# Gated panels of three feed-forward blocks transposed by DMA in two 16-bit planes instead of by TensorE, with two adaLN weight streams moved later

## The chip, the cores and the metric

The kernel runs on one core of one Trainium2 chip. The metric is the device time of one execution in microseconds (us). The core has five engines that each work through their own queue in a fixed order: TensorE (PE in the profile, with its weight loads as PEld), VectorE (DVE), ScalarE (ACT), GpSimd (POOL) and SyncE (SP). SP issues nearly all DMAs here. A queue's order is fixed when the program is built. An instruction that must wait holds up everything behind it on its own engine.

## What is computed

The program is a two-layer diffusion backbone over 256 latent tokens (with 256 context tokens in the first feed-forward block and the attention), width 1024, hidden width 2816, float32:

```python
def modulate(x, shift, scale):
    return x * (1 + scale) + shift

def swiglu_ffn(h, w_in, w_out):
    a, u = jnp.split(h @ w_in, 2, axis=-1)
    return (jax.nn.silu(a) * u) @ w_out

def half_step_ffn(x, shift, scale, gate, w_in, w_out, g, b):
    y = swiglu_ffn(modulate(x, shift, scale), w_in, w_out)
    return post_norm_update(x, y, gate, 0.5, g, b)     # LayerNorm(alpha * x + 0.5 * gate * y)
```

Each layer is a feed-forward half step, a token mixer (attention in layer 0, a short gated convolution in layer 1) and a second feed-forward half step. The nine modulation vectors of a layer come from `silu(c) @ ada_w[i] + ada_b[i]`.

## The kernel before, in words

**Precision.** Every float32 matrix product is made of three products of split operands. A number is split into a part `hi` that TensorE takes at its fast rate and the rest `lo = x - hi`, and hi·hi, hi·lo and lo·hi are summed. So each weight that lands from HBM (`w1r`, `w2r`: raw) is split by one ScalarE copy into `w1h` or `w2h` (line 211) and one VectorE subtraction into `w1l` or `w2l` (line 214). A *unit* is 256 rows by 512 columns of weights, 512 KB, and is split in two halves, so in two instructions on each engine.

**A feed-forward block (`ffn`).** Three of the four blocks go through `ffn`: the second of layer 0 (block A here), the first of layer 1 (B) and the second of layer 1 (C). A block has two stages.

The *panel stage* multiplies the modulated tokens by `ffn_w_in` in 11 panels of 256 hidden columns, with 4 units to a panel and two token tiles t = 0, 1 of 128 tokens. A *step* is one unit times one token tile: six matmuls of 128x512. `panels` calls `tick()` after every step; all clocks of the program count steps. The panel stage has 88 steps. When a panel of a token tile is complete, `gated.done` takes `silu` on ScalarE (line 494) and multiplies by the other half on VectorE (line 495), into a tile `sil` with tokens on the partitions. The next product needs the hidden columns on the partitions. So, four steps (`G_LAG`) after both token tiles of a panel are done, `rest` transposes the panel with four TensorE transposes of 128x128 into a PSUM bank `gT` (line 503), and `finish` splits that bank into `gh` (ScalarE, line 113) and `gl` (VectorE, line 114).

The *output stage* multiplies these by `ffn_w_out` in 22 units (two column halves of 11). Its 44 steps are put in order by `order_skew`: token tile 1 follows tile 0 at a distance of five units. Counting steps of this stage from 0, unit u is first used at step 2u-5 (from u = 5 on) and last used at step 2u+6. At the stage's end come the residual (`res`), the layer norm and the transposes for the next block.

**Buffers.** There are four raw unit buffers, five pairs `hi`/`lo` in a pool of the whole program, and as many further pairs as `ext[0]` says. It is 3 in blocks A, B, C and the convolution, so that 8 pairs are used in turn: unit u can be split once unit u-8 has been used for the last time.

**The modulation streams (`ada`).** Background generators load `ada_w` in row blocks of 512 KB (`ar`, three buffers, line 316 on SP), and VectorE adds each, times a column of `silu(c)`, to a sum `acc` in two halves (lines 295 and 297). After eight blocks GpSimd sums over the partitions (`red`, line 307) and adds the result to a row in HBM (`scr`, line 308). `set_background(gen, rate, hold)` makes `rate` generator steps per step of the product, after `hold` steps. A stream of two vectors has 17 such steps. Block A runs the stream for vectors 4 and 5 of layer 1 (rate 0.35, hold 20), block B that for 6 and 7 (rate 0.25), block C that for 8 (rate 0.15). `drain()` runs what is left of a stream. `fold_cols` reads such rows back from `scr` into a small tile `mrow` (line 376, on SP) for the next layer norm but one.

**What sets the order.** TensorE's order is the program's. The other queues are ordered by a list scheduler from priorities when the program is built, so an instruction may stand there long before or after its place in the program. `Late(n, fn)` runs `fn` n steps later. `queued(ins)` places an instruction behind given ones of its queue.

Of the kernel before, what the change touches and what calls it, by code (L numbers as in the profile page):

```python
# [11 lines left out]
F32R = mybir.dt.float32r  # L12
AF = mybir.ActivationFunctionType
# [41 lines left out]
G_LAG = 4  # L55
ROPE_EARLY = 70
# [11 lines left out]
HOLD = 20  # L68
# [3 lines left out]
def backbone_kernel(  # L72
# [19 lines left out]
    w_early = [0]  # L92
    ext = [1, 0]
# [86 lines left out]
    def wunit(srcs, kn, s, own=None, wd=512, put_off=False):  # L180
# [23 lines left out]
        with tc.high_priority(offset=w_early[0]):  # L204
            for src, c in srcs:
                sync.dma_start(rv[:, :, c:c + src.shape[2]], src)

        def parts():
            m = kn * wd
            for a in range(0, m, m // W_HI):  # L210
                nc.scalar.activation(hi[:, a:a + m // W_HI], raw[:, a:a + m // W_HI], AF.Copy)  # L211
            for a in range(0, m, m // W_LO):
                b = a + m // W_LO
                nc.vector.tensor_tensor(out=lo[:, a:b], in0=raw[:, a:b], in1=hi[:, a:b].bitcast(F32), op=ALU.subtract)  # L214
            return hv, lv
# [268 lines left out]
    def run(gen):  # L484
        for _ in gen:
            pass

    def gated(func, finish, s):

        part, res = {}, []  # L490

        def done(p, t, bk):
            g = sp.tile([P, 256], F32, tag="s2", bufs=S2, name=nm("sil"))
            nc.scalar.activation(g, bk[:, 0:256], func)
            gate_ins[:] = [nc.vector.tensor_tensor(out=g, in0=g, in1=bk[:, 256:512], op=ALU.mult)]
            part[p, t] = g
# [344 lines left out]
    def ffn(hTs, later, l, j, i, gm, nxt, own=()):  # L841
# [5 lines left out]
        done, gT = gated(AF.Silu, finish, "gT")  # L847
# [7 lines left out]
        drain()  # L855
# [334 lines left out]
    run(panels(cols, w, hTs, lead_in(6), done, "wc"))  # L1190
    g, hTs, later = sub_end(sc_w_out[0], lhs_T(yT), KC, 1, 1, 5, 1.0, (1, 6), "wo", order_late(KU))
# [57 lines left out]
```

## Time and profile before

| | |
|---|---|
| median of 3 runs | 1258.37 us (1257.19 to 1258.66) |
| the profiled execution's own time | 1258.45 us |
| its span in the trace | 1256.7 us |
| granted TensorE clock over the span | 0.998 of full speed |
| block A: panel stage, output stage | from 592.1 us, from 718.35 us |
| block B: panel stage, output stage | from 780.2 us, from 906.4 us |
| block C: panel stage, output stage | from 1062.7 us, from 1188.5 us |

The profiled execution lies 0.08 us above the median and 1.75 us above its span. The page gives the busy time of each engine, the span in 40 slices, the chain of instructions that ended last, and the costliest groups of instructions. The groups' rows have line, engine, operation, output<-inputs, shape and count, then the busy time in us and the mean of one in ns, then the engine's idle time just before them and what ended it. Rows of the timeline have start and length in us, then the engine, line and operation with a count; idle time before it stands in square brackets, with what ended it. Rows by windows have the busy time of PE, PEld, DVE, ACT and POOL, the granted clock, the busy share of the DMA engines and GB/s.

### The profile page before, as it was taken

To read this page: it belongs to the slowest core of one execution; us is meant where nothing else is said; L and a number is where in the kernel's file an instruction comes from. 1 tells how busy PE (TensorE), PEld (TensorE's weight loads), DVE (VectorE), ACT (ScalarE), POOL (GpSimd) and SP (SyncE) were. 2 spreads that over 40 slices of the span, in tenths; PEclk is the share of its full clock that TensorE was granted. 3 is DMA by queue.
4 is the path that set the end of the run, shared out by engine and by line. 5 is a ranking of instruction groups with operands and counts; after the bars stand their busy time and mean duration, and the time that the engine had idled before them with its cause. 6 is when DMAs were issued, how large, how long until landed. Compare 5 with 4: busy or idle time off the path is not lost.

```text
span 1256.7 us, 17284 instructions
## 1 busy us (share of the span) xinstructions
PE 1241.4 (99%) x5902; PEld 1006.9 (80%) x5902; DVE 966.5 (77%) x1675; ACT 590.2 (47%) x1152; POOL 85.0 (7%) x83
## 2 busy tenths in 40 slices
PE   8999999999999999999999999999999999999997
PEld 6787778778878878777888888888888887888886
DVE  3599987888878877789899646998646788878546
ACT  2432132312326556688655435655435744655431
POOL 0000000000001111120003100021100000002000
PEclk9999999999999999999999999999999999999999
DMA  9976678788842744455899645889645764885641
GB/s 308 299 235 226 197 236 290 265 260 274 285 156 85 216 94 87 99 115 179 259 335 318 231 150 167 274 293 321 224 146 167 245 206 134 259 290 185 227 159 53
DMA packets 202928, 268.59 MB, mean 214 GB/s; under 512 B 30246, under 2 KB 149534, under 8 KB 202840
## 3 DMA queue, kind: packets, MB, share of 16 engines
q1 hardware_dynamic: 202644, 267.46, 67.4%
q8 instruction: 46, 0.75, 0.2%
q14 instruction: 42, 0.34, 0.1%
q0 software_dynamic: 160, 0.02, 0.0%
q10 hardware_dynamic: 36, 0.02, 0.0%
HBM read 265.27 MB, written 2.20 MB: 213 GB/s over the span
## 4 chain that ended last, share of the span: by engine, by line
PE 92%; ACT 3%; DVE 3%; issue 1%; DMA 1%; POOL 0%; DVEq 0%; SPq 0%; POOLq 0%; ACTq 0%
PE f L695 19%; PE w L165 17%; PE w L168 17%; PE w L166 17%; PE wkv L165 2%; PE wkv L166 2%; PE wkv L168 2%; PE wc L165 2%; PE wc L168 2%; PE wc L166 2%; PE gT L503 1%; PE ada L624 1%; PE hT L437 1%; PE S L987 1%; PE wo L165 1%
## 5 line engine op out<-in xcount | busy, mean ns | idle before, releaser
L211 ACT ACTIVATE w1h<-w1r 128x512 fp32r<-128x512 f32 (+1 forms) x352 | 200.0, 620 | 180.0 <-PE w L168 81.5
L214 DVE TENSOR_TENSOR w1l<-w1r,w1h 128x512 fp32r<-128x512 f32 (+1 forms) x352 | 241.7, 734 | 35.5 <-ACT w1h L211 33.2
L165 PE MATMUL w<-w1h,hTh 128*128 128x512 f32 x528 | 209.1, 396 | 1.3 <-ACT hTh L113 1.3
L166 PE MATMUL w<-w1l,hTh 128*128 128x512 f32 x528 | 205.9, 390 | 0.3 <-DVE w1l L214 0.3
L297 DVE SCALAR_TENSOR_TENSOR acc<-ar,cst,acc 128x512 f32<-128x512 f32 x266 | 186.2, 747 | 15.3 <-DMA ar<-in_ada_w_dram 15.3
L165 PE MATMUL w<-w2h,gh 128*128 128x512 f32 (+1 forms) x446 | 173.4, 389 | 0.0
L166 PE MATMUL w<-w2l,gh 128*128 128x512 f32 (+1 forms) x446 | 172.1, 387 | 0.0
L211 ACT ACTIVATE w2h<-w2r 128x512 fp32r<-128x512 f32 x176 | 101.5, 624 | 145.2 <-PE w L168 106.5
L214 DVE TENSOR_TENSOR w2l<-w2r,w2h 128x512 fp32r<-128x512 f32 x176 | 114.1, 688 | 72.0 <-ACT w2h L211 71.2
L168 PE MATMUL w<-w1h,hTl 128*128 128x512 f32 x528 | 163.1, 390 | 0.2 <-DVE hTl L114 0.2
L168 PE MATMUL w<-w2h,gl 128*128 128x512 f32 (+1 forms) x446 | 136.1, 386 | 0.0
L695 PE MATMUL f<-h0h,w1h 128*128 128x512 f32 x352 | 133.1, 394 | 0.4 <-DVE h0h L650 0.4
L695 PE MATMUL f<-h0l,w1h 128*128 128x512 f32 x352 | 133.2, 391 | 0.0
L695 PE MATMUL f<-h0h,w1l 128*128 128x512 f32 x352 | 132.7, 390 | 0.0
L165 PEld LDWEIGHTS w<-w1h,hTh 128*128 128x128 f32 x528 | 99.2, 188 | 21.8 <-ACT hTh L113 2.1
L168 PEld LDWEIGHTS w<-w1h,hTl 128*128 128x128 f32 x528 | 98.9, 188 | 22.0 <-DVE hTl L114 1.0
L166 PEld LDWEIGHTS w<-w1l,hTh 128*128 128x128 f32 x528 | 99.2, 188 | 20.4 <-DVE w1l L214 0.7
L165 PEld LDWEIGHTS w<-w2h,gh 128*128 128x128 f32 x446 | 83.8, 188 | 19.3 <-issue 1.7
L166 PEld LDWEIGHTS w<-w2l,gh 128*128 128x128 f32 x446 | 83.8, 188 | 16.6
L168 PEld LDWEIGHTS w<-w2h,gl 128*128 128x128 f32 x446 | 83.3, 188 | 17.1
L695 PEld LDWEIGHTS f<-h0h,w1h 128*128 128x128 f32 x352 | 65.7, 188 | 19.0 <-issue 4.2
L695 PEld LDWEIGHTS f<-h0l,w1h 128*128 128x128 f32 x352 | 65.5, 188 | 14.4 <-issue 0.8
(189 smaller groups left out, 1719.6 us busy)
## 6 DMA issues: line engine op xcount, KB each, us to landing
w1r<-in_ffn_w_in_dram SPq DMA_DIRECT2D x340, 256.0 KB
ar<-in_ada_w_dram SPq DMA_DIRECT2D x128, 512.0 KB
w2r<-in_ffn_w_out_dram SPq DMA_DIRECT2D x88, 512.0 KB
ar<-in_ada_w_dram SPq DMA_DIRECT2D x32, 256.0 KB
wkvr<-in_na_w_qkv_dram SPq DMA_DIRECT2D x32, 256.0 KB
wcr<-in_sc_w_in_dram SPq DMA_DIRECT2D x32, 256.0 KB
wqr<-in_na_w_qkv_dram SPq DMA_DIRECT2D x8, 512.0 KB
wor<-in_na_w_out_dram SPq DMA_DIRECT2D x8, 512.0 KB
```

Source lines behind the costliest of these rows:

```text
L165: nc.tensor.matmul(ps, lh, rh, start=first and i == 0, stop=False)
L166: nc.tensor.matmul(ps, lh, rl, start=False, stop=False)
L168: nc.tensor.matmul(ps, ll, rh, start=False, stop=last and i == n - 1)
L211: nc.scalar.activation(hi[:, a:a + m // W_HI], raw[:, a:a + m // W_HI], AF.Copy)
L214: nc.vector.tensor_tensor(out=lo[:, a:b], in0=raw[:, a:b], in1=hi[:, a:b].bitcast(F32), op=ALU.subtract)
L297: nc.vector.scalar_tensor_tensor(out=a, in0=src, scalar=sc, in1=a, op0=ALU.mult, op1=ALU.add)
L437: nc.tensor.transpose(ps[:, k * P:(k + 1) * P], z[h][:, k * P:(k + 1) * P], ident)
L503: nc.tensor.transpose(ps[:, j * 256 + i * P:j * 256 + (i + 1) * P], g[:, j * P:(j + 1) * P], ident)
L624: nc.tensor.matmul(ps[o:o + 32, 0:m], cst[:, a * kt + i, :], w[:, i, j, :], start=(a == 0 and i < 2), stop=(a == last and i >= kt - 2))
L695: nc.tensor.matmul(ps, w, hT0[k][part == 1], start=(k == part == 0), stop=(k == KC - 1 and part == 1))
L987: nc.tensor.matmul(banks[i], (qh, qh, ql)[f][ps, qs], (kh, kl, kh)[f][ps, :], start=f == 0, stop=f == 2)
```

## The change

In `ffn`, panels 0 to 8 of the eleven (`BY_DMA = NP - 2`) no longer use TensorE for the transpose; panels 9 and 10 still do. For each token tile of such a panel, ScalarE copies the gated tile, seen as 16-bit words, into a tile `hal` in which all low halves stand before all high halves (128x512 words of 16 bits). Eight steps later (`T_LAG`, in the program's order) SP issues a transposing DMA of that tile into `halT`, from SBUF to SBUF, placed behind the last weight load issued so far (`last_load`). Fourteen steps after the panel (`D_LAG`) ScalarE puts the two planes together again into a float32 tile `gTw` (128x1024 words), placed behind the last weight split so far (`last_split`); `finish` then splits `gTw` instead of a PSUM bank. For three blocks that is 27 panels: 108 TensorE transposes go, and 54 plane copies, 54 DMAs and 27 joins come. The convolution's `gated` is unchanged (`by_dma` is 0).

The streams of A and B start at step 70 (`HOLD`) with rates 0.4 and 0.3, and are no longer drained ahead of the output stage but after the block (A) or after the convolution's panels (B). `ext[0]` falls from 3 to 2 for A, B, C and the convolution, so that 7 pairs are used in turn.

```diff
+T_LAG = 8
+D_LAG = 14
+BY_DMA = NP - 2
...
-HOLD = 20
+HOLD = 70
...
-                sync.dma_start(rv[:, :, c:c + src.shape[2]], src)
+                last_load[:] = [sync.dma_start(rv[:, :, c:c + src.shape[2]], src)]
...
+            if p < by_dma:
+                if t == 0:
+                    part[p] = hp.tile([P, 4, 256], U16, tag="halT", bufs=2, name=nm("halT"))
+                halves = hp.tile([P, 2, 256], U16, tag="hal", bufs=4, name=nm("hal"))
+                nc.scalar.activation(halves, g.bitcast(U16).rearrange("p (f s) -> p s f", s=2), AF.Copy)
+
+                def turn():
+                    with queued(last_load):
+                        sync.dma_start_transpose(part[p][:, :, t * P:(t + 1) * P], halves.rearrange("p s f -> p (s f)"))
+
+                turns.append(Late(T_LAG, turn))
+                if t == 1:
+                    mine = turns[-2:]
+
+                    def joined():
+                        for turn in mine:
+                            turn.get()
+                        w = sp.tile([P, 512], F32, tag="tmp", bufs=3, name=nm("gTw"))
+                        with queued(last_split):
+                            nc.scalar.activation(w.bitcast(U16).rearrange("p (f s) -> p s f", s=2),
+                                                 part.pop(p).rearrange("p (s j) n -> p s (j n)", s=2), AF.Copy)
+                        return finish(p, w)
+
+                    res.append(Late(D_LAG, joined))
+                return
...
-        done, gT = gated(AF.Silu, finish, "gT")
+        done, gT = gated(AF.Silu, finish, "gT", BY_DMA)
...
-        drain()
+        if made_here:
+            drain()
...
-    ext[0] = 3
-
-    set_background(stream([(1, 4, 0), (1, 5, 0)]), 0.35, HOLD)
-    hTs, later = ffn(hTs, later, 0, 1, 2, 8, (1, 0), own)
-
-    set_background(stream([(1, 6, 0), (1, 7, 0)]), 0.25)
-    hTs, later = ffn(hTs, later, 1, 0, 0, 2, (1, 3))
+    ext[0] = 2
+
+    set_background(stream([(1, 4, 0), (1, 5, 0)]), 0.4, HOLD)
+    hTs, later = ffn(hTs, later, 0, 1, 2, 8, (1, 0), own, False)
+    drain()
+
+    set_background(stream([(1, 6, 0), (1, 7, 0)]), 0.3, HOLD)
+    hTs, later = ffn(hTs, later, 1, 0, 0, 2, (1, 3), (), False)
```

**What moves on the queues.** First, ScalarE through one panel in the middle of block A's panel stage, before (`sil` is the gated tile, `w1h` a unit's split, `gh` the split of the transposed panel, each with its number in the program):

```order
L494 ACTIVATE sil_1107_5945<-w1_1091_5837 128x256
L211 ACTIVATE w1h_1147_6135<-w1r_1146_6134 128x512 x2
L494 ACTIVATE sil_1108_5954<-w1_1097_5887 128x256
L211 ACTIVATE w1h_1151_6160<-w1r_1150_6159 128x512 x2
L113 ACTIVATE gh_1122_6016<-gT_1121_6011 128x512
L211 ACTIVATE w1h_1157_6191<-w1r_1156_6190 128x512 x2
L211 ACTIVATE w1h_1162_6214<-w1r_1161_6213 128x512 x2
```

ScalarE through one panel of the same stage after the change:

```order
L499 ACTIVATE sil_1155_6168<-w1_1141_6090 128x256
L505 ACTIVATE hal_1157_6172<-sil_1155_6168 128x512
L499 ACTIVATE sil_1158_6181<-w1_1142_6097 128x256
L216 ACTIVATE w1h_1191_6336<-w1r_1190_6335 128x512 x2
L505 ACTIVATE hal_1159_6184<-sil_1158_6181 128x512
L216 ACTIVATE w1h_1197_6364<-w1r_1196_6363 128x512 x2
L520 ACTIVATE gTw_1193_6350<-halT_1156_6171 128x2x512
L118 ACTIVATE gh_1194_6352<-gTw_1193_6350 128x512
L216 ACTIVATE w1h_1205_6397<-w1r_1204_6396 128x512 x2
L216 ACTIVATE w1h_1210_6420<-w1r_1209_6419 128x512 x2
```

Two plane copies and a join are new, and the join `gTw` stands one unit's split behind the second plane copy of the same panel.

Second, SP at the place where it reads back the first sum of block A's stream (`mrow<-scr1`; DMASW0 is the semaphore of GpSimd's DMA into `scr`), before, in the panel stage:

```order
L206 DMA w1r_1266_6753<-in_ffn_w_in_dram 128x2x256 [waits DMAHW1_49,DVE_49]
L206 DMA w1r_1266_6753<-in_ffn_w_in_dram 128x2x256 [waits DMAHW2_49]
L206 DMA w1r_1271_6776<-in_ffn_w_in_dram 128x2x256 [waits DMAHW3_49,DVE_49]
L206 DMA w1r_1271_6776<-in_ffn_w_in_dram 128x2x256 [waits DMAHW4_49]
L376 DMA mrow_1640_8707<-scr1_117 8x128 [waits DMAHW5_49,DMASW0_49]
L206 DMA w1r_1277_6806<-in_ffn_w_in_dram 128x2x256 [waits DMAHW6_49,DVE_49]
L206 DMA w1r_1277_6806<-in_ffn_w_in_dram 128x2x256 [waits DMAHW7_49]
```

SP at the read-back of the same sum after the change, in block A's output stage (`w2r_1367` is unit 10 of that stage, `w2r_1372` unit 11; `ar_1335` is the eighth block of the stream and `ar_1366` the thirteenth):

```order
L321 DMA ar_1335_7006<-in_ada_w_dram 128x1024 [waits DMAHW0_49,DVE_49]
L211 DMA w2r_1363_7146<-in_ffn_w_out_dram 128x2x512 [waits DMAHW1_49,DVE_49]
L321 DMA ar_1342_7038<-in_ada_w_dram 128x1024 [waits DMAHW2_49,DVE_49]
L211 DMA w2r_1367_7170<-in_ffn_w_out_dram 128x2x512 [waits DMAHW3_49,DVE_49]
L321 DMA ar_1353_7087<-in_ada_w_dram 128x1024 [waits DMAHW4_49,DVE_49]
L321 DMA ar_1358_7112<-in_ada_w_dram 128x1024 [waits DMAHW5_49,DMAHW0_49,DVE_49]
L321 DMA ar_1362_7142<-in_ada_w_dram 128x1024 [waits DMAHW6_49,DMAHW2_49,DVE_49]
L381 DMA mrow_1680_8725<-scr1_117 8x128 [waits DMAHW7_49,DMASW0_49]
L381 DMA mrow_1919_9977<-in_ln_g_dram 8x128 [waits PE_49]
L211 DMA w2r_1372_7195<-in_ffn_w_out_dram 128x2x512 [waits DMAHW1_49,DVE_49]
L321 DMA ar_1366_7166<-in_ada_w_dram 128x1024 [waits DMAHW4_49,DVE_49]
```

The read-back of the sum (`mrow_1680`) has moved from the panel stage into the output stage. It stands four rows behind the load of unit 10; directly behind it stand a row of the layer norm, the load of unit 11 and the load of the stream's thirteenth block.

Third, VectorE in block A's output stage before (units 8 to 12; `w2l` is a unit's split):

```order
L214 TENSOR_TENSOR w2l_1340_7114<-w2r_1338_7112,w2h_1339_7113 128x512 x2
L214 TENSOR_TENSOR w2l_1343_7134<-w2r_1341_7132,w2h_1342_7133 128x512 x2
L214 TENSOR_TENSOR w2l_1346_7154<-w2r_1344_7152,w2h_1345_7153 128x512 x2
L214 TENSOR_TENSOR w2l_1351_7179<-w2r_1349_7177,w2h_1350_7178 128x512 x2
L214 TENSOR_TENSOR w2l_1355_7200<-w2r_1353_7198,w2h_1354_7199 128x512 x2
```

VectorE in the same stage after the change (units 8, 9 and 10 are `w2l_1361`, `w2l_1365` and `w2l_1369`; `acc_1354` is the stream's second sum):

```order
L302 SCALAR_TENSOR_TENSOR acc_1354_7089<-ar_1358_7112,cst_89,acc_1354_7089 128x512 x2
L219 TENSOR_TENSOR w2l_1361_7124<-w2r_1359_7122,w2h_1360_7123 128x512 x2
L302 SCALAR_TENSOR_TENSOR acc_1354_7089<-ar_1362_7142,cst_89,acc_1354_7089 128x512 x2
L219 TENSOR_TENSOR w2l_1365_7148<-w2r_1363_7146,w2h_1364_7147 128x512 x2
L302 SCALAR_TENSOR_TENSOR acc_1354_7089<-ar_1366_7166,cst_89,acc_1354_7089 128x512 x2
L219 TENSOR_TENSOR w2l_1369_7172<-w2r_1367_7170,w2h_1368_7171 128x512 x2
```

Each unit's split now has a pair of additions of the stream ahead of it; the addition of `ar_1366` stands ahead of the split of unit 10.

More of the change, by code (lines that the diff above doesn't have):

```diff
@@ L12 @@
 F32R = mybir.dt.float32r
+U16 = mybir.dt.uint16
 AF = mybir.ActivationFunctionType
@@ L486, in run, with gated @@
             pass
-    def gated(func, finish, s):
-        part, res = {}, []
+    def gated(func, finish, s, by_dma=0):
+        part, res, turns = {}, [], []
         def done(p, t, bk):
@@ L839, in lhs_T, with ffn @@
         return f
-    def ffn(hTs, later, l, j, i, gm, nxt, own=()):
+    def ffn(hTs, later, l, j, i, gm, nxt, own=(), made_here=True):
         def finish(p, ps):
@@ L1190, in backbone_kernel @@
     run(panels(cols, w, hTs, lead_in(6), done, "wc"))
+    drain()
     g, hTs, later = sub_end(sc_w_out[0], lhs_T(yT), KC, 1, 1, 5, 1.0, (1, 6), "wo", order_late(KU))
```

3 lines of the change are left out of this document (2 added, 1 removed).

## The prediction

> **What bounds the kernel now.** I read the page first: part 1 for the busy engine, part 4 for what the chain that ended last is made of.
>
> ```profile
> span 1256.7 us, 17284 instructions
> PE 1241.4 (99%) x5902; PEld 1006.9 (80%) x5902; DVE 966.5 (77%) x1675; ACT 590.2 (47%) x1152; POOL 85.0 (7%) x83
> PE 92%; ACT 3%; DVE 3%; issue 1%; DMA 1%; POOL 0%; DVEq 0%; SPq 0%; POOLq 0%; ACTq 0%
> ```
>
> TensorE is busy 99% of the span and makes up 92% of the chain. So a transpose that leaves TensorE counts in full, and any wait put into TensorE counts in full. Next I asked by windows for block A: six panels (from the transposes of one panel to those of the sixth after it), a busy stretch of the panel stage, and a stretch of the output stage.
>
> ```profile
> 642.88:711.06 68.18, 68.18 (x314) 56.41 (x313) 62.69 (x95) 35.17 (x66) 17.92 (x5) 1.00 0.87 297
> 620.00:660.00 40.00, 40.00 (x186) 33.09 (x185) 36.76 (x64) 22.10 (x42) 2.76 (x1) 1.00 0.91 308
> 740.00:760.00 20.00, 20.00 (x90) 16.57 (x89) 13.27 (x21) 9.03 (x16) 0.00 (x0) 1.00 0.56 186
> ```
>
> TensorE has no gap in any of them. In the panel stage VectorE is at 92% (62.69 of 68.18) and DMA at 0.87; in the output stage they are at 66% and 0.56, and ScalarE at 45%. That is the room into which the change moves the streams.
>
> **The transposes.** A panel takes 68.18 / 6 = 11.36 us. What four units take without transposes shows in the output stage, where ScalarE's splits are paced by TensorE (they wait for `w L168`, the last use of a buffer pair). From the first to the last of these rows are three units.
>
> ```profile
> 642.88 0.60 PE L503 MATMUL gT<-ident,sil 128*128 128x128 f32 x4
> 654.25 0.60 PE L503 MATMUL gT<-ident,sil 128*128 128x128 f32 x4
> 728.94 1.15 ACT L211 ACTIVATE w2h<-w2r 128x512 fp32r<-128x512 f32 x2 [5.28 <-PE w L168]
> 737.12 1.15 ACT L211 ACTIVATE w2h<-w2r 128x512 fp32r<-128x512 f32 x2 [1.56 <-PE w L168]
> ```
>
> 8.18 us for three units is 2.73 a unit and 1.363 a step; four units are 10.91. The difference, 11.36 - 10.91 = 0.46 us to a panel, is less than the 0.60 us of the four transposes, which overlap their neighbours. 27 panels give -12.4 us; nothing on TensorE replaces them.
>
> **Block A's read-back (the largest cost).** In block A the stream now starts at step 70 of 88, so its first sum ends in the output stage. Its read-back `mrow` stands on SP ahead of the loads of unit 11 and of the stream's block `ar_1366`, and must wait for GpSimd's sum and write. VectorE adds `ar_1366` ahead of the split of unit 10. So TensorE can wait at unit 10 for: sum, GpSimd, SP, a load, an addition, a split. The rows for its links:
>
> ```profile
> 718.35 0.39 PE L165 MATMUL w<-w2h,gh 128*128 128x512 f32 x1
> 718.96 0.42 DVE L495 TENSOR_TENSOR sil<-sil,w 128x256 f32<-128x256 f32 x1 [0.84 <-ACT sil L494]
> 640.89 2.73 DVE L297 SCALAR_TENSOR_TENSOR acc<-ar,cst,acc 128x512 f32<-128x512 f32 x4
> 729.61 1.29 DVE L214 TENSOR_TENSOR w2l<-w2r,w2h 128x512 fp32r<-128x512 f32 x2 [1.58 <-ACT w2h L211]
> L114 DVE TENSOR_TENSOR gl<-gT,gh x33: 677/686/693, 614.4 to 1193.8; 128x512 fp32r<-128x512 f32 x33
> 832.74 7.66 POOL L307 PARTITION_ALL_REDUCE red<-acc  x1 [47.81 <-DVE acc L297]
> 840.70 1.00 POOL L308 DMA_DIRECT2D scr<-red  x1 [0.30 <-POOL red L307]
> 844.98 0.30 SPq L376 DMA_DIRECT2D mrow<-scr  x1
> SPq L376 <- DMA scr<-red: 5.6, 2, 3.4
> 727.07 0.24 PE L380 MATMUL mcT<-ident,mrow 32*128 32x32 f32 x1
> 633.94 3.46 SPq L206 DMA_DIRECT2D w1r<-in_ffn_w_in_dram  x5
> 638.36 1.15 ACT L211 ACTIVATE w1h<-w1r 128x512 fp32r<-128x512 f32 x2 [3.65 <-DMA w1r<-in_ffn_w_in_dram]
> 815.46 3.62 SPq L206 DMA_DIRECT2D w1r<-in_ffn_w_in_dram  x6
> 821.37 1.15 ACT L211 ACTIVATE w1h<-w1r 128x512 fp32r<-128x512 f32 x2 [5.55 <-DMA w1r<-in_ffn_w_in_dram]
> ```
>
> Time from the first matmul of the output stage (718.35). The last gated product ends at +1.03 (718.96 + 0.42). Behind it VectorE's order has six half additions at 0.68 (2.73 / 4), a unit's split of 1.29 and a `gl` of 0.69 before the sum is complete: +7.1. From GpSimd's start to SP's read-back it took 12.24 us (832.74 to 844.98): +19.3. SP then issues two small rows, unit 11 and `ar_1366`, by its rows about 0.3 each, 1.0 together: +20.3. A load of 512 KB was used 4.4 us after its issue (633.94 to 638.36) or 5.9 us after (815.46 to 821.37); I take the middle, 5.2, since DMA is emptier in this stage than in either: +25.5. The addition takes 1.37, the first half of unit 10's split 0.65: +27.5. TensorE needs that half at the stage's step 2 x 10 - 5 = 15: 15 x 1.363, plus 0.46 for panel 10's transposes, 0.3 for a small transpose of `mcT` (0.24 in its row), and 0.23 for the second matmul, where `lo` comes in: +21.4. The wait is 6.1 us. Behind it VectorE has an addition and a split for each unit (1.37 + 1.29 = 2.66) against TensorE's 2.73, so nothing is regained and about 0.9 is added by the second half: **+7.0**, between 4 (a load in 4.4, VectorE 1.5 earlier) and 8.5.
>
> **Block B.** There the sums come later (rate 0.3), and the read-back of vector 7 can keep SP for some 8 of those 12.24 us from unit 21's load, which four raw buffers (4 x 2.73 = 10.9 us) just cover. VectorE's load is 66% plus 0.3 x 1.37 / 1.363 = 30%, so 96%: small waits. I take +0.7, from 0 to 3.
>
> **Seven pairs.** A pair is freed two steps (2.73 us) ahead of its next first use instead of four; ScalarE's half and VectorE's split need 0.6 + 1.29 = 1.9. Cost nothing while VectorE is on time; if it is not, this is where TensorE waits (third rival).
>
> **Transposing DMAs and ScalarE.** ScalarE's work to a panel becomes, from these rows: two `silu` of 0.38, two plane copies taken as `gh`, 0.60, four splits of 1.15, a join of 1.03 (two widths of 0.21 to 256 columns above 0.60), one `gh` of 0.60.
>
> ```profile
> L494 ACT ACTIVATE sil<-w x66: 362/384/386, 598.5 to 1188.7; 128x256 f32<-128x256 f32 x66
> L495 DVE TENSOR_TENSOR sil<-sil,w x66: 406/416/422, 600.8 to 1189.1; 128x256 f32<-128x256 f32 x66
> L113 ACT ACTIVATE gh<-gT x33: 578/598/603, 613.7 to 1193.2; 128x512 fp32r<-128x512 f32 x33
> ```
>
> That is 8.2 us, with 0.5 of waiting for the gated product (0.42) 8.7 of 10.91. The join stands one split (1.15) behind the second plane copy, and everything behind it, the next splits above all, waits until both DMAs have landed. So a DMA may take L = 2.2 + 1.15 = 3.35 us from that copy before ScalarE falls behind. With seven pairs, one in use, ScalarE can be six units ahead (16.4 us, less 2 for a split under way: 14.4), spread over nine panels 1.6: TensorE doesn't wait up to L = 4.95. No transposing DMA is in the trace. The nearest rows are the loads: of 4.4 to 5.9 us, 384 KB more at 308 GB/s (the window 620 to 660) are 1.3, so L = 3.1 to 4.6; it has no bank of HBM to read, but it moves 16-bit words. I take 3.6 and **0**. Beyond 4.95 it costs 3 x (9 (L - 3.35) - 14.4). The Trainium skill ("DMA: Bandwidth & Descriptors", section "Latency and other measured facts") gives 261 GB/s for a transposing DMA, by which 128 KB would take an estimated 0.5 us more than an empty transfer; no run here shows it, and the sum would stay.
>
> **At nothing.** SP's 54 issues (0.3 to 0.7 us each by the rows above, about one us of a panel), and the four loads behind them: hidden by the same 14 us lead, lost if L is long. The streams' loads leave the panel stage, where TensorE did not wait for them: no gain. Block C has no moved stream and gains its full 4.1. The drain behind the convolution's panels has little left: 17 steps at 0.3 end at step 127 of 132 in block B.
>
> **Sum.** Against the profiled execution's 1258.45 (0.08 above the median): 1258.45 - 12.4 + 7.0 + 0.7 = **1253.8 us**.
>
> **Rivals.** *First: slow transposing DMAs (ends slower).* ScalarE blocks at each join, splits come late, TensorE waits at every panel once the lead of 14.4 us is gone. At L = 5.5 the loss is 3 x (9 x 2.15 - 14.4) = 14.9: 1268.7; at 5.9, the slowest load, 25.7: 1279. It decides from L = 5.1, where 3 x 1.55 eats what the sum gains. For it: a load under full DMA took 5.9, SP can be at an earlier load when the planes are ready, and 16-bit copies with a stride may take longer than the 0.60 taken (at 1.15 each and 2.1 for the join, ScalarE has nothing free). Against: DMA falls below 0.87 in this stage without the stream. The Trainium skill ("VectorE: DVE Perf Modes", section "The three transpose paths") gives 1309 ns for DMA against 390 ns for TensorE per 128x128 block of 16 bits, and its rules ask for TensorE where PSUM will do; four blocks would be an estimated 5.2 us, and the time about 1262. Here four TensorE transposes cost 0.46 us of the path, and no run yet shows the DMA's.
>
> *Second: the read-back holds nobody up.* If the chain above is 6 us shorter (GpSimd's 12.24 stands on one sum, its span on the page is rough, and the longest wait of SP for it was 3.4), the load of `ar_1366` comes in time: 1258.45 - 12.4 + 0.7 = 1246.8.
>
> *Third: VectorE eats all of it.* In block A it has 66% plus 0.4 x 1.37 / 1.363 = 40%, 106%, for the 24 steps until the stream ends: 24 x 1.363 x 0.06 = 2.0 more; with two steps of lead in both blocks, and B's upper end, 2.3 more: 1258.
>
> **How the numbers follow.** The forecast, with its own range 1250 to 1257.6 from the bounds of A and B, has 0.42; slow DMAs 0.23; no hold-up 0.18; VectorE 0.17. 0.2% is 2.5 us, about what a measurement of this kernel can tell from no change. Faster: 0.38 of the forecast and all of the second rival, 0.56. Same: 0.04 of the forecast, 0.13 of the third, 0.02 of the first, 0.19. Slower: the rest, 0.25. The range goes from under the second rival, 1245.5, to 1270, a little above the middle of the first; above it lies 0.11, below it 0.03, and some of the third's tail.
>
> **What would show it.** Right: a panel period of 10.9 us in all three blocks; one wait of TensorE near +21 us in block A's output stage, before unit 10, for `w2l`, with VectorE waiting for `ar` and SP for `scr` ahead of it; joins on ScalarE that wait under 2.2 us each. Wrong: waits for DMA at `gTw` over 3 us, with TensorE waiting for `w1h` in the panel stages (first rival); no wait near +21 (second); many short ones for `w2l` throughout the output stages of A and B (third).

## The result and the profile after

The changed kernel takes 1294.53 us (median of four runs, 1291.18 to 1296.94) against 1258.42 us before: a ratio of 1.0287, 95% interval 1.0262 to 1.0312. It is 36 us slower, where 4.7 us less were forecast, and lies above the stated range (1245.5 to 1270). The profiled execution is the fastest of the four, 1291.18 us.

The page of the changed kernel, in the order of the lines shown of before: the span and the busy engines, then the chain that ended last.

```profile
span 1289.4 us, 17231 instructions
PE 1239.4 (96%) x5794; PEld 1000.9 (78%) x5794; DVE 964.9 (75%) x1675; ACT 645.3 (50%) x1233; POOL 79.5 (6%) x83
PE 56%; DVE 16%; DMA 12%; ACT 8%; issue 5%; SPq 1%; POOL 0%; DVEq 0%; ACTq 0%; POOLq 0%
```

TensorE is no longer busy throughout, and the chain now runs over VectorE, DMA and ScalarE for a third of the span. ScalarE has 55 us more work and is still busy for only half of the span: what counts is how it waits. By stage (windows from each stage's first matmul to the next stage's: block A's panel stage and output stage, B's two, C's panel stage; busy time of PE, PEld, DVE, ACT, POOL, granted clock, DMA share, GB/s):

```profile
591.10:722.30 131.20, 124.40 (x540) 102.20 (x541) 88.42 (x153) 89.83 (x165) 1.08 (x2) 0.96 0.85 237
722.30:793.20 70.90, 64.77 (x278) 51.35 (x277) 57.02 (x83) 26.92 (x51) 16.43 (x7) 0.98 0.74 250
793.20:920.30 127.10, 123.01 (x541) 101.28 (x540) 84.30 (x147) 88.41 (x163) 1.08 (x2) 0.99 0.82 225
920.40:992.80 72.40, 64.47 (x278) 51.38 (x277) 57.86 (x86) 26.88 (x51) 16.67 (x7) 0.95 0.77 255
1087.90:1220.60 132.70, 124.31 (x540) 102.09 (x541) 94.90 (x157) 88.73 (x164) 8.71 (x5) 0.96 0.82 231
```

Each of the five stages lost time, and each has gaps on TensorE. In numbers:

| stage | before | forecast | after | lost | longest waits of TensorE |
|---|---|---|---|---|---|
| A, panels | 126.2 | 122.1 | 131.2 | +5.0 | 6.7 at panel 9 |
| A, output | 61.8 | 68.8 | 70.9 | +9.1 | 2.9, 1.5, 1.7 |
| B, panels | 126.2 | 122.1 | 127.1 | +0.9 | 4.1 at panel 9 |
| B, output | 61.9 | 62.6 | 72.5 | +10.6 | 6.0, 1.5 |
| C, panels | 125.8 | 121.7 | 132.8 | +7.0 | 8.1 at panel 9 |
| C, output | 60.7 | 60.7 | 60.7 | 0 | none |

The losses add up to 32.6 us, which is the growth of the span (32.7). Two different things happen.

**The panel stages.** The waits of the whole run show who stands where (us in total, times, longest):

```profile
ACT gTw L520 <- DMA halT<-hal: 58.3, 22, 4.2
PE gT L533 <- DVE sil L500: 18.9, 3, 8.1
```

22 of 27 joins stand at the head of ScalarE's queue until their DMAs have landed, 2.65 us on average. For weights TensorE waits hardly at all in these stages (0.3 us, once). It waits three times, once in each block, at the transposes of panel 9: the first panel that it still transposes itself. The last cycle of block A on ScalarE, with TensorE's wait below it:

```profile
699.74 0.36 ACT L499 ACTIVATE sil<-w 128x256 f32<-128x256 f32 x1
...
703.09 0.62 ACT L505 ACTIVATE hal<-sil 128x512 uint16<-128x512 uint16 x1
703.61 1.14 ACT L216 ACTIVATE w1h<-w1r 128x512 fp32r<-128x512 f32 x2
704.65 1.14 ACT L216 ACTIVATE w2h<-w2r 128x512 fp32r<-128x512 f32 x2
708.82 1.34 ACT L520 ACTIVATE gTw<-halT 128x1024 uint16<-128x1024 uint16 x1 [3.03 <-DMA halT<-hal]
710.03 1.12 ACT L216 ACTIVATE w2h<-w2r 128x512 fp32r<-128x512 f32 x2
711.06 0.63 ACT L499 ACTIVATE sil<-w 128x256 f32<-128x256 f32 x2
```
```profile
712.35 0.90 PE L533 MATMUL gT<-ident,sil 128*128 128x128 f32 x3 [6.72 <-DVE sil L500]
```

From the `silu` of panel 8 (699.74) to that of panel 9 (711.06) are 11.32 us, against TensorE's 10.91. ScalarE falls behind with each panel, the `silu` of panel 9 stands behind the join of panel 8, and the transposes four steps after panel 9 find nothing to transpose. From the end of a panel's last matmul to the `silu` of its token tile 1, block A's trace has 2.8 us at panel 0 (as in the kernel before), 6.0 at panel 2, 7.6 at panel 4 and 11.1 at panel 8; before the change it is 0.04 from panel 4 on. So half of the lateness is there after three panels, and the rest grows by some 0.9 us a panel.

**The output stages.** VectorE beside the start of block A's second sum, and GpSimd in the same stretch:

```profile
730.58 6.27 DVE L300 TENSOR_SCALAR acc<-ar,cst 128x512 f32<-128x512 f32 x2 [0.40 <-DMA ar<-in_ada_w_dram]
736.77 0.17 DVE L387 COPY gcol<-mcT 128x32 f32<-128x32 f32 x1
...
737.34 0.75 DVE L302 SCALAR_TENSOR_TENSOR acc<-ar,cst,acc 128x512 f32<-128x512 f32 x1
```
```profile
730.44 6.13 POOL L312 PARTITION_ALL_REDUCE red<-acc  x1 [134.14 <-DVE acc L302]
```

Two multiplications of 0.48 us took 6.27 us together: they end 0.3 us behind GpSimd's sum (736.6). The split of unit 7 stands behind them, and TensorE waits 2.87 us for its `w2l` until 738.74. In block B it is a product of two small columns that stands still beside the first sum, 4.5 us instead of 0.16; the split of unit 7 is behind it again, and the wait is 6.0 us.

```profile
934.26 4.52 DVE L390 TENSOR_TENSOR gcol<-gcol 128x8 f32<-128x8 f32 x1
```

**What a wait costs besides.** The clock that the throttle grants falls behind a long wait (windows: the wait in block A's panel stage and the matmuls behind it, then the same in C):

```profile
704.00:711.50 7.50, 1.62 (x8) 1.01 (x6) 5.16 (x9) 4.47 (x9) 0.00 (x0) 0.75 1.13 274
711.50:717.00 5.50, 4.65 (x13) 3.84 (x14) 5.50 (x11) 4.01 (x9) 0.00 (x0) 0.50 0.96 337
1202.20:1210.80 8.60, 0.47 (x3) 0.08 (x2) 5.09 (x10) 6.39 (x13) 0.00 (x0) 0.72 0.81 212
1210.80:1216.00 5.20, 5.20 (x15) 4.19 (x16) 4.71 (x9) 3.35 (x7) 0.00 (x0) 0.50 0.89 308
```

At 0.50 a matmul starts every 427 ns instead of every 227. The 5 to 6 us at that clock cost 2.3 us more behind the wait of 6.7 us in A's panels and 2.3 behind that of 8.1 us in C's; the wait of 2.9 us in A's output stage cost 1.5 more. Hence the losses in the table are larger than the waits less the 4.1 us gained.

### The profile page after: what moved, and what is told of

It is laid out like the page before. It is cut to its first block, busy times and chain, and to the rows that moved or that the text cites. A ratio compares the mean times of both kernels' runs of the same rounds, so it can differ in the third digit from the quotient of the medians.

```text
span 1289.4 us, 17231 instructions
## 1 busy us (share of the span) xinstructions
PE 1239.4 (96%) x5794; PEld 1000.9 (78%) x5794; DVE 964.9 (75%) x1675; ACT 645.3 (50%) x1233; POOL 79.5 (6%) x83
## 3 DMA queue, kind: packets, MB, share of 16 engines
q1 hardware_dynamic: 232020, 274.54, 70.9%
## 4 chain that ended last, share of the span: by engine, by line
PE 56%; DVE 16%; DMA 12%; ACT 8%; issue 5%; SPq 1%; POOL 0%; DVEq 0%; ACTq 0%; POOLq 0%
PE f L725 19%; PE w L171 7%; PE w L173 7%; PE w L170 7%; DVE w1l L219 6%; DMA w1r<-in_ffn_w_in_dram 6%; DMA halT<-hal 2%; DMA ar<-in_ada_w_dram 2%; DVE w2l L219 2%; ACT w1h L216 2%; PE wc L170 2%; PE wc L171 2%; PE wc L173 2%; DVE acc L302 2%; PE wkv L170 1%
## 5 line engine op out<-in xcount | busy, mean ns | idle before, releaser
L219 DVE TENSOR_TENSOR w1l<-w1r,w1h 128x512 fp32r<-128x512 f32 (+1 forms) x352 | 226.9, 690 | 34.9 <-ACT w1h L216 32.9
L171 PE MATMUL w<-w2l,gh 128*128 128x512 f32 (+1 forms) x446 | 174.9, 393 | 14.1 <-DVE w2l L219 14.0
L219 DVE TENSOR_TENSOR w2l<-w2r,w2h 128x512 fp32r<-128x512 f32 x176 | 119.8, 719 | 48.6 <-ACT w2h L216 48.3
L725 PE MATMUL f<-h0h,w1h 128*128 128x512 f32 x352 | 132.8, 393 | 1.1 <-ACT w1h L216 0.6
L170 PEld LDWEIGHTS w<-w2h,gh 128*128 128x128 f32 x446 | 84.6, 190 | 19.3 <-issue 1.7
L725 PEld LDWEIGHTS f<-h0h,w1h 128*128 128x128 f32 x352 | 65.5, 188 | 19.4 <-issue 4.2
```

Source lines behind the costliest of these rows:

```text
L170: nc.tensor.matmul(ps, lh, rh, start=first and i == 0, stop=False)
L171: nc.tensor.matmul(ps, lh, rl, start=False, stop=False)
L725: nc.tensor.matmul(ps, w, hT0[k][part == 1], start=(k == part == 0), stop=(k == KC - 1 and part == 1))
```

## The experiments

All are timed beside the kernel before, and each ratio is to it. First the two halves of the change apart, and a cut into each. The diffs are against the changed kernel.

**Transposes alone** (streams as before; seven pairs stay, since the tiles of 16-bit words fill the room of the eighth):

```diff
-HOLD = 70
+HOLD = 20
...
-    set_background(stream([(1, 4, 0), (1, 5, 0)]), 0.4, HOLD)
-    hTs, later = ffn(hTs, later, 0, 1, 2, 8, (1, 0), own, False)
-    drain()
+    set_background(stream([(1, 4, 0), (1, 5, 0)]), 0.35, HOLD)
+    hTs, later = ffn(hTs, later, 0, 1, 2, 8, (1, 0), own)
...
```

> The DMA transposes alone: streams as before (rates 0.35 and 0.25, drained ahead of the output stage), seven pairs. Theory Q (ScalarE's queue is over-full: each join holds it 2 to 4 us for its DMAs, so silu comes later from panel to panel, until TensorE stands at the transposes of panel 9, the first that it still makes itself, four steps after that panel): in each of the three blocks one TensorE wait of 4 to 8 us there, panel stages of 127 to 133 us against 126.4 before, output stages of A and B at 62 as before; time 1266 to 1278. Theory M (the streams that start at step 70 crowd VectorE and the DMA queues, and this makes panel 9 late in A and B): no such wait in A and B, only block C's 8 us; time about 1257.

Measured: 1302.55 us, ratio 1.0344 (1.0327 to 1.0361). Output stages 61.8 and 61.9 as before; panel stages 141.2, 148.5 and 133.1, with waits at panel 9 of 9.5, 12.9 and 8.0 us. Theory M is refuted: streams in the panel stage make it worse, so moving them out had helped there. Theory Q has the right place, but A and B lose more than it said; more on that below.

**Streams alone** (all transposes on TensorE, eight pairs), **and the same without the sums:**

```diff
-BY_DMA = NP - 2
+BY_DMA = 0
...
-    ext[0] = 2
+    ext[0] = 3
```

> The moved streams alone: all transposes on TensorE, eight pairs, streams from step 70 at 0.4 and 0.3. Theory H (while GpSimd sums over the partitions, an instruction of VectorE stands still for 4 to 5 us; before, that fell into the panel stage, now it falls into the output stage where TensorE has little lead): TensorE waits begin within a few us of each sum's start, output stages of A and B at 66 to 72 us against 62; time 1266 to 1278. Theory D (the output stages lose because ScalarE comes late out of the panel stage, and because of seven pairs): output stages at 62 to 64; time 1258 to 1262.

> The moved streams alone, and GpSimd's sum over the partitions is left out: GpSimd writes the first partition of each vector's sum to HBM as it stands (for the five vectors of these blocks, so these modulation vectors are other numbers). Loads, additions, the write and SP's read-back stay. Theory H: no instruction of VectorE takes over 2 us, the waits beside the sums go, at most a wait at unit 10 by the load of ar stays; time 1257 to 1262, and at least 8 below the run with the sums. Theory V (VectorE's additions and SP's read-back are too much for the output stage, whatever GpSimd does): within 3 us of the run with the sums.

```diff
-            red = hp.tile([P, D], F32, tag="red", name=nm("red"))
-            nc.gpsimd.partition_all_reduce(red, acc[i], P, ReduceOp.add)
+            red = acc[i]
```

Measured: 1271.29 us with the sums (1.0099, 1.0084 to 1.0114), 1258.59 without (1.0002, 0.9993 to 1.0012). The output stages of A and B by windows, with the sums and without:

```profile
718.10:784.00 65.90, 63.59 (x278) 50.06 (x277) 53.89 (x79) 25.78 (x48) 19.29 (x7) 1.00 0.77 270
910.10:978.70 68.60, 63.79 (x278) 50.05 (x277) 56.63 (x83) 25.77 (x49) 17.87 (x7) 1.00 0.78 263
```
```profile
718.10:779.80 61.70, 61.70 (x278) 50.73 (x277) 46.89 (x79) 25.84 (x49) 4.46 (x5) 1.00 0.83 284
906.40:968.50 62.10, 62.10 (x278) 50.50 (x277) 48.67 (x83) 25.75 (x49) 3.23 (x5) 1.00 0.84 288
```

Without the sums TensorE has no gap in these stages, with the same loads, additions and read-backs; VectorE is busy for 7 and 8 us less, at the same number of instructions. The row at the place of the stall, without the sum:

```profile
726.09 0.88 DVE L300 TENSOR_SCALAR acc<-ar,cst 128x512 f32<-128x512 f32 x2 [1.13 <-DMA ar<-in_ada_w_dram]
```

Theory V falls: with eight pairs VectorE has room for the stream. Theory H has the time right, but the run without sums takes away two things at once: VectorE's standing, and the 6 to 9 us by which the sum delays SP's read-back. The trace with the sums shows both at work. In block A there is no wait beside the first sum; the only ones over 0.2 us (1.65 and 0.47 us, at units 11 and 12) come 11 us after its end, where VectorE waits for an `ar` that was loaded behind the read-back. Block B waits 0.85 us right behind the first sum, and 2.73 us at the end of the stage: SP had stood for 8 us at the read-back of the second sum, with the convolution's weights behind it.

```profile
951.56 0.37 SPq L211 DMA_DIRECT2D w2r<-in_ffn_w_out_dram  x1
960.08 0.30 SPq L381 DMA_DIRECT2D mrow<-scr  x1
960.42 0.35 SPq L321 DMA_DIRECT2D ar<-in_ada_w_dram  x1
960.87 9.81 SPq L211 DMA_DIRECT2D wcr<-in_sc_w_in_dram  x6
```

How much each of the two costs is not measured apart. Moving the streams gains nothing by itself either: 1258.59 is the time of before.

**The place of TensorE's own transposes** (transposes alone):

```diff
+G_LATE = 12
...
-    def gated(func, finish, s, by_dma=0):
+    def gated(func, finish, s, by_dma=0, lag=G_LAG):
...
-                res.append(Late(G_LAG, rest))
+                res.append(Late(lag, rest))
...
-        done, gT = gated(AF.Silu, finish, "gT", BY_DMA)
+        done, gT = gated(AF.Silu, finish, "gT", BY_DMA, G_LATE)
```

> The DMA transposes alone as in the first of these runs, but TensorE's own transposes of panels 9 and 10 stand 12 steps after their panel instead of 4 (their results are first needed at steps 13 and 15 of the output stage). Theory Q: the three waits go and nothing takes their place, panel stages of 122 to 123 us in all three blocks; time 1246 to 1250. Rival (ScalarE is so late that the splits of the output stage's first units are late too): TensorE waits for w2h or w2l instead, 3 us or more in each block; time 1257 or more.

Measured: 1279.45 us (1.0167, 1.0151 to 1.0184), 23 us under the run before it. The waits at panel 9 are gone: block C's panel stage is 121.5 us. But C's output stage went from 60.7 to 66.5, A's and B's to 65 and 65.5, and the panel stages of A and B are still 128.4 and 134.8 us, with many short waits for `w1l`: ScalarE is still late, and part of the lateness shows one stage on. Theory Q has the place of the waits right, the rival what follows.

**The joins' waiting.** The DMAs are left out, and the join reads the plane copies:

```diff
-                    with queued(last_load):
-                        sync.dma_start_transpose(...)
+                    part[p].append(halves)
...
+                            for i, hv in enumerate(part.pop(p)):
+                                nc.scalar.activation(w[:, i * 256:(i + 1) * 256].bitcast(U16)..., hv, AF.Copy)
```

> The DMA transposes alone (streams as before), but the transposing DMAs are left out: the join reads the plane copies as they stand, in two instructions of 128x512 words, so the output stage multiplies by untransposed panels. ScalarE keeps its added work and loses the waiting. Theory W (what makes ScalarE's queue over-full is the waiting of each join for its DMAs): a panel is 9.0 us of work on ScalarE against TensorE's 10.9, no wait of TensorE at panel 9, panel stages of 122 to 123 us, time 1246 to 1250. Theory R (the added copies and joins alone are too much for ScalarE): at least half of the waits stay, time 1275 or more.

Measured: 1245.13 us (0.9891, 0.9875 to 0.9908), just below what theory W said. The three panel stages by windows:

```profile
593.70:715.20 121.50, 121.43 (x540) 100.21 (x541) 109.03 (x176) 90.53 (x174) 22.30 (x7) 1.00 0.89 297
777.20:898.30 121.10, 121.10 (x541) 100.08 (x540) 104.87 (x172) 88.29 (x171) 22.43 (x7) 1.00 0.85 278
1055.20:1176.40 121.20, 121.20 (x540) 100.26 (x541) 95.12 (x157) 89.73 (x173) 8.98 (x5) 1.00 0.75 235
```

ScalarE does as much work as in the changed kernel (90, 88 and 90 us), the streams run in the panel stages, and TensorE hardly waits. So it is not the added work. The run takes away two things at once, though: the joins' waiting, and SP's standing at the transposing DMAs. The runs with longer lags, below, tell these apart.

**Four panels instead of nine** (`BY_DMA = 4`, streams as before):

> The DMA transposes alone, for panels 0 to 3 only; panels 4 to 10 on TensorE. Theory Q (ScalarE falls behind a little in each such panel): the wait stands at the transposes of panel 4 now and is 0 to 4 us, after that ScalarE catches up; TensorE saves 12 x 0.46 = 5.5 us; time 1253 to 1266. Rival (it is the change-over itself from DMA panels to TensorE panels that costs, however many there are): waits of 8 to 13 us at panel 4; time 1280 or more.

Measured: 1274.78 us (1.0129, 1.0114 to 1.0145), between the two. Waits at panel 4 of 4.3, 7.6 and 3.5 us. In C, where little else goes on, 3.5 us after four panels and 8.0 after nine (transposes alone) are 0.9 us to a panel. The four steps until TensorE needs the panel are 5.5 us, so ScalarE was about 9 late after four, and some 5 of these do not come from falling behind panel by panel. They are the lateness of the first three panels; where that comes from stays open.

**Later joins**, and then both lags:

```diff
-T_LAG = 8
-D_LAG = 14
+T_LAG = 6
+D_LAG = 18
...
-tag="halT", bufs=2
+tag="halT", bufs=3
...
-tag="hal", bufs=4
+tag="hal", bufs=2
```

> The DMA transposes alone, all nine panels; the join stands about three splits (3.4 us) behind the second plane copy in ScalarE's queue instead of one (D_LAG 18, T_LAG 6, three tiles halT, two hal). Theory W: the joins wait under 1.5 us each, ScalarE's cycle falls below TensorE's, the waits at panel 9 fall to under 3 us in each block; time 1248 to 1262. Theory R (work, not waiting): they stay over 6 us; time 1285 or more.

> As the run with late joins, and TensorE's own transposes of panels 9 and 10 stand 12 steps after their panel instead of 4. Theory W with Q: no wait of TensorE over 1 us in the panel stages, 122 to 124 us each; time 1246 to 1252, below the kernel before. Rival (lateness moves on into the output stage): time 1258 or more, with waits for w2h, w2l or gh at the start of the output stages.

Measured: 1293.39 us (1.0274, 1.0254 to 1.0295) with late joins, 1267.51 us (1.0076, 1.0054 to 1.0097) with both: the times that theory R and the rival gave, but not by their mechanisms. Block C behaved as theory W has it: 121.3 us with 60.7 behind it, and 120.8 with 61.2 when both are late, 182.0 either way, so that the late joins alone are enough there. A and B did not: 140.6 and 147.2, then 128.6 and 129.9. Of the joins only 12 wait now in each run, but other waits stand in their place. ScalarE in block A with late joins, and SP:

```profile
671.94 2.18 ACT L216 ACTIVATE w1h<-w1r 128x512 fp32r<-128x512 f32 x4
679.65 1.15 ACT L216 ACTIVATE w1h<-w1r 128x512 fp32r<-128x512 f32 x2 [5.53 <-DMA w1r<-in_ffn_w_in_dram]
680.71 1.34 ACT L520 ACTIVATE gTw<-halT 128x1024 uint16<-128x1024 uint16 x1
```
```profile
663.66 1.54 SPq L211 DMA_DIRECT2D w1r<-in_ffn_w_in_dram  x3
671.13 3.02 SPq L509 DMA_TRANSPOSE halT<-hal  x2
674.24 0.53 SPq L321 DMA_DIRECT2D ar<-in_ada_w_dram  x1
674.83 1.45 SPq L211 DMA_DIRECT2D w1r<-in_ffn_w_in_dram  x3
```

SP issues nothing from 665.2 to 671.1: it stands at a transposing DMA whose plane copy is not made, with the weight loads behind it, and ScalarE then waits 5.5 us for such a load. A late ScalarE can thus make itself later. So three more runs took the streams or the sums out.

**The whole change with both lags, with and without sums; the change as it is without sums:**

> The whole change with late joins and late TensorE transposes. Theory W with Q (panel stages) and H (output stages): panel stages of 121 to 123 us in all three blocks, since no stream crowds them; output stages of A and B still at 66 to 72 us; time 1256 to 1266. Theory S (SP stands at a transposing DMA until the plane copy is made, with the weight loads behind it; that alone keeps ScalarE late): panel stages of A and B at 126 or more; time 1268 or more.

> As the run before it, and GpSimd's sum over the partitions is left out: it writes the first partition of each sum as it stands (other modulation vectors). W, Q and H together: output stages of A and B at 62 to 63 us, panel stages at 121 to 123; time 1244 to 1248, all of the 12.4 us that TensorE saves. If something else holds the output stages: 1252 or more.

> The whole change as it is, with GpSimd's sum over the partitions left out (other modulation vectors). Theory H: output stages of A and B at 62 to 64 us, panel stages as in the changed kernel (131, 127, 133) with their waits at panel 9; time 1271 to 1278. If the output stages are late because ScalarE comes late out of the panel stage: they stay at 67 or more; time 1285 or more.

| GpSimd's sums | lags as changed | both lags longer |
|---|---|---|
| made | 1294.53 | 1266.46 (1.0057, 1.0042 to 1.0072) |
| left out | 1276.82 (1.0137, 1.0119 to 1.0156) | 1249.76 (0.9924, 0.9909 to 0.9939) |

The two causes nearly add: 28.1 us by the lags, 17.7 by the sums, 44.8 by both. With both lags the panel stages of all three blocks are 120.6 to 121.2 us, with the sums and without. Theory S alone falls by that, since SP stands at the transposing DMAs no less than before: with both lags and the sums made, 46 of the 54 start within 0.03 us of the end of their plane copy, and SP had issued nothing for 37.8 us ahead of them in all; in the changed kernel these are 42 and 37.5 us. One of them with both lags, the plane copy and SP:

```profile
672.68 0.63 ACT L506 ACTIVATE hal<-sil 128x512 uint16<-128x512 uint16 x1 [0.98 <-DVE sil L501]
673.33 3.02 SPq L510 DMA_TRANSPOSE halT<-hal  x2
```

What the lags took away is ScalarE's waiting at the joins: 20.5 us instead of 58.3. With the sums made the output stages of A and B are 73.6 and 72.4 us although ScalarE is on time, a little more than expected; so it is not a late ScalarE that holds them. The change as it is without sums kept its waits at panel 9 (6.3 to 6.6 us), as expected. The last run's 1249.76 lies between its two forecasts, 3.8 us above the 1246.0 that the sum without any wait gives; its output stages of 63.3 and 64.0 us, against 61.8, hold 3.6 of them, with longest waits of 0.4 and 1.1 us.

**What remains in A and B when the stream is in the panel stage:**

> Streams as before (in the panel stages of A and B), DMA transposes with late joins and late TensorE transposes as in the run with both, and GpSimd's sum over the partitions left out (other modulation vectors). That run had panel stages of 129.6 and 130.1 us in A and B and 121.0 in C. Theory H (it is the sum's hold on VectorE that throws A and B out of step, after which SP stands at the transposing DMAs): 121 to 123 us in A and B too; time 1245 to 1250. Theory S (the stream's loads and additions with SP's stand at the transposing DMAs do it): 126 or more in A and B; time 1257 or more.

Measured: 1262.40 us (1.0028, 1.0018 to 1.0038); A 125.3 with 66.1 behind it, B 127.6. That is nearer theory S. Against the run with both (128.6 and 129.9 by its trace) leaving out the sums took 3.3 and 2.4 us off the panel stages, not 8. The larger part comes from the stream's loads and additions together with the DMA transposes; SP's standing at the transposing DMAs is 30 to 33 us in each of A and B in these two runs, against 9 to 14 in the runs that have the streams moved. Whether the loads or the additions do it stays open.

**Versions that transpose by DMA where no stream runs:** block C alone, then B and C with B's stream in the convolution.

> DMA transposes in block C alone, with late joins and late TensorE transposes as in the run with both; A and B transpose on TensorE, streams as before, seven pairs. Theory W with Q: block C's stages at 121 and 61 us as in that run (4.4 us under the kernel before together), A and B as before; time 1252 to 1255. Rival (seven pairs, or the lower DMA traffic of this run's A and B, take something back): 1257 or more.

> DMA transposes in blocks B and C (late joins, late TensorE transposes), A as before; block B's stream runs in the convolution's panel stage instead, at 0.45. If a panel stage without a stream is what the DMA transposes need: block B's panel stage 121 us, C's 121, the convolution within 1 us of 70.1; time 1247 to 1251. If the convolution has no room for the stream and its two sums: its stages are 4 us longer or more; time 1253 or more.

```diff
-        done, gT = gated(AF.Silu, finish, "gT", BY_DMA)
+        done, gT = gated(AF.Silu, finish, "gT", 0 if nxt else BY_DMA, G_LAG if nxt else G_LATE)
```

Block C alone: 1253.74 us, 0.9959 (0.9944 to 0.9974): faster than both kernels. C's panel stage by windows:

```profile
1062.70:1183.40 120.70, 120.70 (x537) 99.86 (x537) 91.29 (x151) 85.54 (x158) 8.70 (x5) 1.00 0.87 252
```

B and C: 1261.27 us (1.0017, 1.0008 to 1.0027), so the second forecast held. B's panel stage is 120.7 us without its stream, as expected. But the first sum of B's stream now begins in B's output stage, at 921.3 us; that stage lost 5.5 us and the convolution's second stage 10, with waits of 3.0 and 3.6 us. The stream has no free place there either.

## Why the prediction was wrong

**The saving on TensorE was right.** 12.4 us were forecast; the run without the DMAs is 13.5 below before, and the panel stages of all runs without waits are 120.6 to 121.6 us.

**The time of a transposing DMA was right, what it costs was not.** L was put at 3.6 us. In the 22 panels whose join waits, it is 2.7 to 5.2 us from the end of the second plane copy to the join, median 3.6; since L was the middle of a guess from loads, that it fits to a tenth is partly luck. The sizes beside it were somewhat low:

```profile
L505 ACT ACTIVATE hal<-sil x54: 615/630/672, 600.9 to 1202.1; 128x512 uint16<-128x512 uint16 x54
L520 ACT ACTIVATE gTw<-halT x27: 1341/1365/1374, 613.7 to 1206.0; 128x1024 uint16<-128x1024 uint16 x27
L509 SPq DMA_TRANSPOSE halT<-hal x54: 1188/1195/1681, 601.6 to 1202.8; - x54
```

With 0.63 and 1.37 ScalarE's work is 8.6 us to a panel, and with 0.5 and a wait of 2.65 it is 11.7 against 10.91: about 0.8 late per panel, as block C shows (0.9). To this come, in block A, 2.8 us at panel 0 (as before the change) and 3.2 more by panel 2 that no term explains. The forecast had seen such lateness and let ScalarE's lead of six units, 14.4 us, hide it: "TensorE doesn't wait up to L = 4.95". **This is the step that failed.** The six units are the lead of the weights. `silu` has no such lead: it can only start when TensorE has finished the panel, and TensorE wants the result four steps (5.5 us) later, at the first panel that it transposes itself. It stands in the same queue as the joins, so that is where the lateness arrives: 18.9 us of waits at panel 9 of the three blocks, and panel stages that took 12.9 us more in place of 12.4 less. The first rival named the mechanism, ScalarE blocked at each join, and priced it with the same 14.4 us; at the measured L it would have cost nothing.

**The rule against the change.** The Trainium skill ("VectorE: DVE Perf Modes", section "Rules for kernel authors") asks for TensorE where PSUM will do. The runs bear it out for A and B. The 5.2 us for four blocks, estimated from the 1309 ns of that page's section "The three transpose paths", did not come: the median here is 3.6. Block C alone goes against the rule, by 5.6 us in the medians (3.3 to 7.1 by the interval).

**Block A's read-back came as forecast, with a stall inside it.** The +7.0 us came out as +9.1. From the stage's start GpSimd's sum begins at +8.1 us (forecast +7.1), SP reads it back at +18.3 (+19.3), VectorE waits for `ar` until +25.7 (+25.5), and the second matmul of unit 10 begins at +27.8 (+27.5).

```profile
748.03 1.42 DVE L302 SCALAR_TENSOR_TENSOR acc<-ar,cst,acc 128x512 f32<-128x512 f32 x2 [3.03 <-DMA ar<-in_ada_w_dram]
```

TensorE waits only 1.5 us there, because it is late already: it had waited 2.9 us at unit 7, from +13.5, and lost 1.5 at half clock. **This is the second step that failed:** the sum had taken GpSimd's 12.24 us as time that passes on GpSimd and SP alone, and put what VectorE does meanwhile at nothing. Up to unit 10 that is hidden inside the forecast wait; beside the second sum it costs 1.7 us more. VectorE's standing was in the trace of before, beside the very sum that the chain was built from (832.74 to 840.40): three splits of 0.69 took 5.63 us together.

```profile
834.93 5.63 DVE L214 TENSOR_TENSOR w1l<-w1r,w1h 128x512 fp32r<-128x512 f32 x3
```

TensorE did not wait there, in a panel stage with eight pairs. The Trainium skill names a possible reason ("GPSIMD Engine Reference", section "1. Specifications": GpSimd shares its way to SBUF with VectorE, which collides with instructions that have two inputs in SBUF or run in a mode of two ports). The instructions that stood are subtractions of two SBUF tiles, a multiplication of one tile and a product of two columns; the runs show that they stand and for how long, not why.

**Block B, seven pairs.** B's +0.7 (0 to 3) came out as +10.6. Here the stall is paid: 6.0 us at unit 7 beside the first sum (about 4.4 by the stall, estimated from the 4.52 us that took 0.16 elsewhere) and 1.5 beside the second. Third rival: VectorE was not full. Without the sums it leaves no wait with eight pairs, and waits of under 1.1 us with seven. The loss of the eighth pair was put at nothing as long as VectorE is on time, and VectorE was not. With eight pairs (streams alone) the output stages of A and B still lose 4.2 and 6.7 us; with seven and ScalarE on time (the whole change with both lags) they lose 11.7 and 10.6. No run has DMA transposes with eight pairs, so what the missing pair costs stays open.

**Block C** was to gain its full 4.1 us because it has no moved stream. It lost 7.0, most of it by its joins: 4.6 are left without GpSimd's sums, one of which falls into this stage. With both lags it gains 4.5 (125.8 + 60.7 against 120.8 + 61.2).

**The half clock** was in no term. Behind each of the changed kernel's five waits of over 2.8 us it took another 1.5 to 2.3 us; with what follows the shorter waits that is some 10 of the 32.7 us by which the span grew.

## What to carry to other kernels

Where work is moved to an engine that has idle time, ask what stands behind it in that engine's queue, and how soon *that* is wanted: an in-order queue hands a wait on to its most urgent instruction, not to the one with the longest lead. A join for a DMA belongs so far behind its issue that it hardly waits, and consumers that are near in time must not stand behind it. Before work is moved between stages, look at how long each kind of instruction takes beside the moved one (maximum against median), since a stall that is free in one stage can be paid in another. An experiment that leaves a piece of work out takes all its effects away at once: it shows that the piece matters, and the trace has to show by which way.

## What the runs showed of the hardware

- While GpSimd sums over the partitions (6.1 to 9.5 us), one instruction of VectorE takes 3.6 to 5 us instead of 0.2 to 0.7, while others beside the same sum run at their usual length; each of the five sums of the kernel before held one for 4.4 to 5 us.
- In the changed kernel the granted clock is 0.50 for 3 to 6 us behind waits of TensorE of 2.9 us and more; behind single waits of under 2 us matmuls came out at full rate or nearly so. It is no sharp bound: the whole change with both lags has the half clock behind waits of 2.2 and 2.5 us, the run with both lags and the streams as before behind 1.5 us with 0.5 close after it, and streams alone does not have it behind one of 2.7 us. The Trainium skill ("TensorE: Matmul & The Clock Gate", section "What's actually happening") has the half clock after about 3.4 us of idling; the traces have the half, also behind waits shorter than that.
- A transposing DMA of 128x512 words of 16 bits occupies SP for 1.2 us, against 0.3 to 0.5 us of most loads' issues.
- A transposing DMA waits on SP for its input, with every load behind it: 42 of the 54 started within 0.03 us of the end of their plane copy.
